# Nearest-neighbour upsampling by two: four equal loads replaced by eight that grow from 1 MiB to 4 MiB

## The chip, the cores and the metric

The kernel runs on one core of a Trainium2 chip, with nothing else running. The metric is the device time of one execution in microseconds (us); quoted times are medians of several runs. All runs quoted here were fast ones, with a granted clock of 1.0 (the share of full TensorE speed that the profile lists), so they may be compared with each other. A difference under 2% counts as "the same".

## The reference

Every element of a 16 x 64 x 64 x 64 array of 32-bit floats is repeated twice in both image directions:

```
result[:, :, i, j] = x[:, :, i // 2, j // 2]     # out: 16 x 64 x 128 x 128
```

There is no arithmetic. The kernel must read 16.78 MB and write 67.11 MB.

## The kernel before

The image rows are cut into four blocks of 128 partitions x 128 rows. A block is loaded by one DMA of 4 MiB: each partition receives one contiguous run of 32 KiB. All four loads are issued at the start, into four buffers. Then each block is expanded in four steps of 32 rows: VectorE writes 18 of the rows, ScalarE 14, into one of two output buffers of 4 MiB, and one store sends it to HBM, again as one contiguous 32 KiB run per partition.

```
K, J = 32, 4
NB = R // (P * J * K)                       # 4 blocks
xpool = ctx.enter_context(tc.tile_pool(name="xin", bufs=NB))
upool = ctx.enter_context(tc.tile_pool(name="uexp", bufs=2))

for n in range(NB):
    xt = xpool.tile([P, J * K, W], fdt, name="xt")
    nc.sync.dma_start(out=xt[:, :, :], in_=xf[n])                    # L67
    xts.append(xt)

for n in range(NB):
    for j in range(J):
        r0 = j * K
        u = upool.tile([P, K, s, W, s], fdt, name="u")
        nc.vector.tensor_copy(out=u[:, :KV], in_=expanded(...))      # L78
        nc.scalar.copy(out=u[:, KV:], in_=expanded(...))             # L81
        nc.sync.dma_start(out=of[n, :, r0 : r0 + K, :], in_=u[...])  # L84
```

Loads and stores are all issued by SyncE, so they all go into one DMA queue, in program order. (The first load is moved in front of the barrier with which the program begins; the change leaves that alone.)

## Time and profile before

| | before |
|---|---|
| time, median of 3 runs | 199.99 us (199.93 to 200.45) |
| span in the profile | 198.2 us |
| DMA queue, share of 16 engines' span | 98.8% |
| VectorE (DVE) / ScalarE (ACT) busy | 21% / 26% |
| VectorE waits for the first load | 12.3 us |

The first thing to read is the page: the busy time of the engines; then the span in 40 equal slices, where each digit is the busy share in tenths (9 is 90% or more); then the DMA packets and the one queue.

```profile
DVE 40.9 (21%) x16; ACT 52.0 (26%) x17; POOL 0.2 (0%) x4
...
DVE  0055000000405050505050505050505050404000
ACT  2057000000415150606060606060606060505000
...
DMA  8999999999999999999999999999999999999994
...
DMA packets 2880, 83.89 MB, mean 423 GB/s; under 512 B 320, under 2 KB 320, under 8 KB 320
...
q1 hardware_dynamic: 2880, 83.89, 98.8%
```

The DMA row is full from the first slice to the last; the two compute engines mostly have nothing to do. Their early digits (slices 3 and 4) are the first two outputs, made at 12 to 19 us. Then both engines stop for 33 us. The waits (engine, line, what it waited for, us in total, times, longest us) and the timeline (start, duration, engine, line, what) of the kernel before say why:

```profile
DVE u L78 <- DMA out_dram<-u: 127.3, 14, 34.7
ACT u L81 <- DMA out_dram<-u: 118.0, 14, 33.5
DVE u L78 <- DMA xt<-in_x_dram: 12.3, 1, 12.3
```

```profile
0.00 2.15 SPq L67 DMA_DIRECT2D xt<-in_x_dram  x4
...
15.55 40.05 SPq L84 DMA_DIRECT2D out_dram<-u  x3
```

All four loads are in the queue at 2.15 us. The first store is issued at 15.55 us, behind all of them, and lands at 52.0 us; only then is an output buffer free again. The copies are waiting for the stores, and the stores for the DMA engines.

The chain that ended last, followed in order of time (start, us, what):

```profile
0.00 12.32 DMA xt<-in_x_dram
...
12.35 6.27 ACT u L81 x2
...
18.63 43.02 DMA out_dram<-u
...
64.96 16.04 DMA out_dram<-u
```

It begins with a wait of 12.32 us for the first load. Its next transfer is a store that takes 43.02 us to land where later ones take 16.04, and most of it is time in the queue behind loads.

The trace's packet records give durations. On each of the 16 DMA engines, packets of 32 KiB take 1,213 ns, one behind the other, in the load stage as in the store stage.

### The profile page before, as it was taken

How to read it: one execution, taken by the hardware profiler on the slowest of the kernel's cores; microseconds unless marked ns; L12 is line 12 of the kernel's file. 1: busy time of each engine (PE TensorE's matmuls, PEld its weight loads, DVE VectorE, ACT ScalarE, POOL GpSimd, SP SyncE). 2: the span in 40 equal slices, each digit the busy share in tenths (PEclk: the TensorE clock that was granted, in tenths of full speed). 3: DMA queues.
4: the chain of work that ended last, by engine and by line, in shares of the span. 5: the costliest groups of instructions: out<-in, count | busy, mean ns of one | idle time of the engine just before them, and what ended most of it. 6: DMA issues, size and time to landing. Idle time of an engine off the chain costs nothing.

```text
span 198.2 us, 145 instructions
## 1 busy us (share of the span) xinstructions
DVE 40.9 (21%) x16; ACT 52.0 (26%) x17; POOL 0.2 (0%) x4
## 2 busy tenths in 40 slices
DVE  0055000000405050505050505050505050404000
ACT  2057000000415150606060606060606060505000
POOL 0000000000000000000000000000000000000000
DMA  8999999999999999999999999999999999999994
GB/s 317 423 423 430 450 430 456 370 403 423 423 423 436 436 443 456 436 436 423 423 423 423 423 443 443 450 450 436 423 423 423 423 423 436 436 443 456 436 436 212
DMA packets 2880, 83.89 MB, mean 423 GB/s; under 512 B 320, under 2 KB 320, under 8 KB 320
## 3 DMA queue, kind: packets, MB, share of 16 engines
q1 hardware_dynamic: 2880, 83.89, 98.8%
HBM read 16.78 MB, written 67.11 MB: 423 GB/s over the span
## 4 chain that ended last, share of the span: by engine, by line
DMA 77%; ACT 14%; issue 0%; ACTq 0%
DMA out_dram<-u 70%; ACT u L81 14%; DMA xt<-in_x_dram 6%; ACTq L81 0%
## 5 line engine op out<-in xcount | busy, mean ns | idle before, releaser
L81 ACT COPY u<-xt 128x3584 f32<-128x3584 f32 x16 | 50.8, 3179 | 128.3 <-DMA out_dram<-u 118.0
L78 DVE COPY u<-xt 128x4608 f32<-128x4608 f32 x16 | 40.9, 2560 | 139.6 <-DMA out_dram<-u 127.3
L81 ACT ACT_TABLE_LOAD x1 | 1.3, 1283 | 0.8 <-PEq L103 0.8
L103 POOL MEMSET const-bfloat16-1.0<- 128x1 bf16 x1 | 0.1, 102 | 0.0
L103 POOL MEMSET const-uint8-127<- 128x1 uint8 x1 | 0.1, 102 | 0.0
L103 POOL MEMSET const-float32-0.0<- 128x1 f32 x1 | 0.1, 99 | 0.2 <-issue 0.2
L103 POOL MEMSET const-float32-1.0<- 128x1 f32 x1 | 0.1, 99 | 0.0
## 6 DMA issues: line engine op xcount, KB each, us to landing
out_dram<-u SPq DMA_DIRECT2D x16, 4096.0 KB, 16.1
xt<-in_x_dram SPq DMA_DIRECT2D x4, 4096.0 KB, 25.9
```

The source lines that it names most:

```text
L78: nc.vector.tensor_copy(out=u[:, :KV], in_=expanded(xts[n][:, r0 : r0 + KV, :]))
L81: nc.scalar.copy(out=u[:, KV:], in_=expanded(xts[n][:, r0 + KV : r0 + K, :]))
L103: nc = _bacc.Bacc("TRN2", target_bir_lowering=False, num_devices=1)
```

## The change

The intent is to let the first copies and the first store start earlier, by making the first loads small (1 MiB, 8 KiB per partition), and to keep the large 32 KiB runs for the last two loads. Core of the diff:

```
+    blocks = [32, 32, 32, 32, 64, 64, 128, 128]      # rows per partition
-    K, J = 32, 4
+    K = 32
...
-    xpool = ctx.enter_context(tc.tile_pool(name="xin", bufs=NB))
+    xpool = ctx.enter_context(tc.tile_pool(name="xin", bufs=1))
...
-    for n in range(NB):
-        xt = xpool.tile([P, J * K, W], fdt, name="xt")
-        nc.sync.dma_start(out=xt[:, :, :], in_=xf[n])
-        xts.append(xt)
+    for n, k in enumerate(blocks):
+        xt = xpool.tile([P, k, W], fdt, name=f"x{n}")     # its own buffer each
+        nc.sync.dma_start(out=xt[:, :, :], in_=of_block(xf, first, k))
+        loaded.append((xt, first, k))
+        first += P * k
...
+    for xt, first, k in loaded:
+        for r0 in range(0, k, K):
             ...                                           # copies and stores as before
```

More of the change, by code (lines that the diff above doesn't have):

```diff
@@ L44 @@
     fdt = x.dtype
-    K, J = 32, 4
-    NB = R // (P * J * K)
-    assert NB * P * J * K == R
-    xf = x.rearrange("b c h w -> (b c h) w").rearrange(
-        "(n p r) w -> n p r w", n=NB, p=P
-    )
-    of = out.rearrange("b c (h hd) w -> (b c h) (hd w)", hd=s).rearrange(
-        "(n p r) w -> n p r w", n=NB, p=P
-    )
-    KV = 18
-    xpool = ctx.enter_context(tc.tile_pool(name="xin", bufs=NB))
-    upool = ctx.enter_context(tc.tile_pool(name="uexp", bufs=2))
-    xts = []
-    for n in range(NB):
-        xt = xpool.tile([P, J * K, W], fdt, name="xt")
-        nc.sync.dma_start(out=xt[:, :, :], in_=xf[n])
-        xts.append(xt)
@@ L70, in expanded, with of_block @@
-    def expanded(rows):
-        k = rows.shape[1]
-        return rows.unsqueeze(2).unsqueeze(4).to_broadcast([P, k, s, W, s])
-    for n in range(NB):
-        for j in range(J):
-            r0 = j * K
+    blocks = [32, 32, 32, 32, 64, 64, 128, 128]
+    K = 32
+    assert P * sum(blocks) == R
+    KV = 18
+    xf = x.rearrange("b c h w -> (b c h) w")
+    of = out.rearrange("b c (h hd) w -> (b c h) (hd w)", hd=s)
+    def of_block(rows, first, k):
+        return rows[first : first + P * k, :].rearrange("(p k) w -> p k w", p=P)
@@ new lines @@
+    xpool = ctx.enter_context(tc.tile_pool(name="xin", bufs=1))
+    upool = ctx.enter_context(tc.tile_pool(name="uexp", bufs=2))
+    loaded = []
+    first = 0
+    for n, k in enumerate(blocks):
[3 more added lines that the diff above has]
+        first += P * k
+    def expanded(rows):
+        return rows.unsqueeze(2).unsqueeze(4).to_broadcast(
+            [P, rows.shape[1], s, W, s]
+        )
@@ L77 @@
+    for xt, first, k in loaded:
+        for r0 in range(0, k, K):
             u = upool.tile([P, K, s, W, s], fdt, name="u")
             nc.vector.tensor_copy(
-                out=u[:, :KV], in_=expanded(xts[n][:, r0 : r0 + KV, :])
+                out=u[:, :KV], in_=expanded(xt[:, r0 : r0 + KV, :])
             )
             nc.scalar.copy(
-                out=u[:, KV:], in_=expanded(xts[n][:, r0 + KV : r0 + K, :])
+                out=u[:, KV:], in_=expanded(xt[:, r0 + KV : r0 + K, :])
@@ L83 @@
             )
             nc.sync.dma_start(
-                out=of[n, :, r0 : r0 + K, :], in_=u[:, :, :, :, :]
+                out=of_block(of, first, k)[:, r0 : r0 + K, :],
+                in_=u[:, :, :, :, :],
             )
```

## The prediction

> **What bounds the kernel.** The DMA engines, from first to last microsecond. The page gives one queue with 98.8% of 16 engines' span, 83.89 MB at 423 GB/s over 198.2 us; VectorE and ScalarE are busy 21% and 26%. The trace's packet records show how full that is: each engine moves 160 packets of 32 KiB back to back at 1,213 ns (16 x 32 KiB / 1.213 us = 432 GB/s), and 20 completion packets of 9 ns. The Trainium skill ("DMA: Bandwidth & Descriptors", "Where 436 GB/s comes from") puts the fabric's ceiling at 435 GB/s; the trace agrees within 1%. What is not transfer at this pace is small: 1.0 to 2.0 us before each engine's first packet, up to 1.1 us more in that packet, about 1.1 us in slower packets at 38 to 40 us, where loads give way to stores, and about 1.5 us after the last packet.
>
> **Loads do not interleave with stores.** All four loads are issued by 2.2 us (timeline), the first store at 15.6 us, on the same queue. The same page ("Queues, rings and completion order") says that each engine takes descriptors in ring order. The trace agrees: the second store, issued at 18.6 us, takes 43.0 us to land (chain of waits), since it stands behind the 16.8 MB of loads; later ones take 16.1 us. So the 12.3 us that VectorE waits for the first load (waits) costs nothing: the DMA engines are full meanwhile, and the first two outputs lie ready over 20 us before the queue reaches them. The chain lists that wait, but its next piece, the 43.0 us store, is mostly queueing.
>
> **What the change does.** Bytes, stores, buffers and copies stay the same. On SyncE the order stays all loads, then all stores; eight loads replace four. The first load is 1 MiB instead of 4. I expect it to land at about 5 us instead of 12.3 (8 packets of about 0.3 us, after 1 to 2 us to the start and the first-packet delay), the first store to be issued at about 9 instead of 15.6 us, and to queue longer by as much. None of these 7 us is on the path that sets the time.
>
> Costs: load packets per engine go from 32 to 64 (32 of 8 KiB, 16 of 16 KiB, 16 of 32 KiB), completion packets from 20 to 24. If each of these 36 more costs what a completion packet takes, 9 ns, they cost 0.3 us (estimate). Four more issues of about 0.4 us on SyncE stay ahead of the transfers.
>
> **Prediction: 200.3 us, range 199.7 to 201.0.** Faster by over 2%: 0.01; within 2%: 0.97; slower by over 2%: 0.02.
>
> **What the profile would show.** If right: DMA again 98 to 99%; 3,456 packets; VectorE's wait for the first load about 5 us; its longest wait for a store grows from 34.7 to about 41 us; the first store still lands near 52 us; later stores still 9.7 us apart; 8 KiB packets at 303 to 312 ns. Wrong, if an 8 KiB packet takes over 330 ns, if there are gaps between loads, or if stores overtake loads.
>
> **What would make it wrong.** A larger cost per descriptor: 8 KiB packets at 350 ns would add 1.5 us. A queue too deep (eight loads and two stores outstanding, against four and two) that leaves engines dry. A transition from loads to stores that costs another amount than 1.1 us. A gain over 1 us would need the start-up or the transition to shrink.

## The result, and the profile after

| | before | after |
|---|---|---|
| time, median of 4 runs | 200.01 us | 200.04 us |
| span in the profile | 198.2 us | 198.2 us |
| VectorE waits for the first load | 12.3 us | 4.9 us |
| first store issued | 15.55 us | 8.15 us |
| last load lands | 42.27 us | 42.52 us |
| first store lands | 51.97 us | 52.20 us |
| last store lands | 197.15 us | 197.40 us |

The ratio is 0.9998, with a 95% interval of 0.9981 to 1.0016: the same. Landings are read from the trace's semaphore events, counted from the start of the span.

The page of the changed kernel:

```profile
DVE 40.9 (21%) x16; ACT 52.1 (26%) x17; POOL 0.2 (0%) x4
...
DVE  0900000000404050505050505050505050504000
ACT  2920000000424151506060606060606060605000
...
DMA  7999999999999999999999999999999999999995
...
DMA packets 3456, 83.89 MB, mean 423 GB/s; under 512 B 384, under 2 KB 384, under 8 KB 384
...
q1 hardware_dynamic: 3456, 83.89, 98.8%
```

The first two outputs moved from slices 3 and 4 to slice 2, as intended. The DMA row, the mean rate and the queue's share did not move. Now its waits, and the beginning of its chain in order of time:

```profile
DVE u L80 <- DMA out_dram<-u: 134.9, 14, 42.4
...
DVE u L80 <- DMA x<-in_x_dram: 4.9, 1, 4.9
```

```profile
0.00 4.92 DMA x<-in_x_dram
...
4.94 3.19 ACT u L83
...
8.15 44.05 DMA out_dram<-u
```

The wait for the load shrank by 7.4 us, and the longest wait for a store grew by 7.7 us, from 34.7 to 42.4. The first store is issued 7.4 us earlier and lands 0.2 us later.

### The profile page after: what moved, and what is told of

Read it like the earlier page. It is cut to its first block, busy times and chain, and to the rows that moved or that the text cites. A ratio compares the mean times of both kernels' runs of the same rounds, so it can differ in the third digit from the quotient of the medians.

```text
span 198.2 us, 155 instructions
## 1 busy us (share of the span) xinstructions
DVE 40.9 (21%) x16; ACT 52.1 (26%) x17; POOL 0.2 (0%) x4
## 2 busy tenths in 40 slices
DMA packets 3456, 83.89 MB, mean 423 GB/s; under 512 B 384, under 2 KB 384, under 8 KB 384
## 3 DMA queue, kind: packets, MB, share of 16 engines
q1 hardware_dynamic: 3456, 83.89, 98.8%
## 4 chain that ended last, share of the span: by engine, by line
DMA 73%; ACT 14%; another core or an unknown queue 3%; issue 0%; ACTq 0%
DMA out_dram<-u 71%; ACT u L83 14%; DMA x<-in_x_dram 2%; ACTq L83 0%
## 5 line engine op out<-in xcount | busy, mean ns | idle before, releaser
L83 ACT COPY u<-x 128x3584 f32<-128x3584 f32 x16 | 50.8, 3179 | 128.5 <-DMA out_dram<-u 125.6
L80 DVE COPY u<-x 128x4608 f32<-128x4608 f32 x16 | 40.9, 2560 | 139.9 <-DMA out_dram<-u 134.9
```

Source lines behind the costliest of these rows:

```text
L80: nc.vector.tensor_copy(out=u[:, :KV], in_=expanded(xt[:, r0 : r0 + KV, :]))
L83: nc.scalar.copy(out=u[:, KV:], in_=expanded(xt[:, r0 + KV : r0 + K, :]))
```

## The experiments

Theory A: the DMA queue always holds work, so the moment at which the first load lands is worth nothing; only engine time counts (packets, idle engines). Its main rival B: the early start does save several us, and the smaller packets cost as much again, so that the two cancel. All numbers on single packets come from the packet records of one profile per kernel; I found out which packets belong to one engine by joining each packet's end to the next one's start.

### The early first load without small packets, and the reverse

Three kernels take the two halves of rival B apart. In the first, the changed kernel's list is turned round: the same packets, but a late first load.

```
-    blocks = [32, 32, 32, 32, 64, 64, 128, 128]
+    blocks = [128, 128, 64, 64, 32, 32, 32, 32]
```

> The changed kernel with its list of blocks reversed (128, 128, 64, 64, 32, 32, 32, 32): same eight loads and the same packets, but the first load is 4 MiB again. Theory A (the DMA queue is never empty, so when the first load lands does not matter; only packets and idle engine time count): the first load lands near 12.3 us instead of 4.9, the first store is issued near 15.5 us, the last load lands near 42.5 us, and the time is that of the changed kernel, 199.9 to 200.4 us. Rival B (the early first load does save several us, and smaller packets give them back): slower than the kernel before by 3 us or more.

Measured: 199.58 us (199.53 to 199.63), ratio to before 0.9978 (0.9965 to 0.9990). Its waits show that the first load is late again:

```profile
DVE u L80 <- DMA out_dram<-u: 127.3, 14, 34.8
...
DVE u L80 <- DMA x<-in_x_dram: 12.1, 1, 12.1
```

Losing the early first load cost nothing, so rival B falls on this side. The kernel even came out 0.4 us below both, just outside what theory A had foreseen; that is taken up further down.

In the second, only the first load is small:

```
-    blocks = [32, 32, 32, 32, 64, 64, 128, 128]
+    blocks = [32, 96, 128, 128, 128]
```

> Only the first load small (blocks 32, 96, 128, 128, 128): the early first load with 32, 24 and 32 KiB packets behind it, so nearly none of the cost of small packets. Theory A: first load at 4.9 us, first store issued near 8 us, time 199.8 to 200.3 us, the same as before. Rival B: faster than before by 3 us or more.

Measured: 200.24 us (200.17 to 200.35), ratio 1.0011 (0.9999 to 1.0024). The first load landed at 4.74 us. The early start by itself gains nothing.

In the third, the kernel before keeps its four loads, but a gap after every 32 rows on chip cuts each run into four of 8 KiB:

```
-        xt = xpool.tile([P, J * K, W], fdt, name="xt")
-        nc.sync.dma_start(out=xt[:, :, :], in_=xf[n])
+        xt = xpool.tile([P, J, K * W + 16], fdt, name="xt")
+        nc.sync.dma_start(out=xt[:, :, : K * W],
+                          in_=xf[n].rearrange("p (j k) w -> p j (k w)", j=J))
```

> The kernel before with the four 4 MiB loads cut into 8 KiB packets (64 bytes of padding after every 32 rows on chip), first load at 12.3 us as before: the supposed cost alone, without the benefit. Theory A: from the changed kernel's packets (309 ns for 8 KiB, 1213 for 32 KiB, each start 3.5 ns before the end of the last) one packet more costs about 4 ns; 96 more per engine cost 0.4 us: 200.2 to 200.7 us. Rival B: 3 us or more slower.

Measured: 200.09 us (199.99 to 200.14), ratio 1.0003 (0.9990 to 1.0015), a little under the expected range. So there was no loss of several us that could have cancelled a gain. From the changed kernel's packets the cost can be read directly: 8, 16 and 32 KiB take 309, 611 and 1,213 ns, each starting 3 to 4 ns before the end of the one before, which leaves a straight line of 37.7 ns per KiB plus 4.6 ns per packet. The changed kernel's 32 extra load packets per engine are then worth 0.15 us, and the 96 of this third kernel 0.44 us. Its time rose by only 0.1 us: in its profile, the packets before the turn from loads to stores were slowed by 0.84 us less than in the kernel before, while the first packets started 0.26 us later (both are in the table further down).

### Much smaller pieces

To be sure that such a cost would be seen, the same trick with a gap after every two rows cuts the loads into pieces of 512 bytes:

```
-        xt = xpool.tile([P, J * K, W], fdt, name="xt")
-        nc.sync.dma_start(out=xt[:, :, :], in_=xf[n])
+        xt = xpool.tile([P, J * K // 2, 2 * W + 8], fdt, name="xt")
+        nc.sync.dma_start(out=xt[:, :, : 2 * W],
+                          in_=xf[n].rearrange("p (g k) w -> p g (k w)", k=2))
 ...        # each copy in two, one for each of the two output rows
```

> The kernel before with the four loads cut into 512-byte packets (32 bytes of padding after every two rows; each copy in two halves): 2048 load packets per engine in place of 32. A straight extension of 4 ns per packet gives 2016 x 4.2 ns = 8.5 us more, 208 to 210 us, and 512-byte packets of about 27 ns. If small packets cost more than the straight line says, the time is over 212 us. In both cases the loss has to be in the load stage, before the last load lands, with stores still 9.7 us apart.

Measured: 215.95 us (215.82 to 215.99), ratio 1.0795 (1.0779 to 1.0812). The straight line was wrong: the loads lost 15.9 us (the last one landed at 58.14 us instead of 42.27), which over 2,016 extra pieces per engine is 7.9 ns apiece and not 4. The trace lumps 16 such pieces into one record of 8 KiB, of typically 436 ns against 309. The stretches of time below (bounds in us, length, busy time of VectorE, ScalarE and GpSimd, clock, DMA share, GB/s) are first those of this kernel, then those of the kernel before:

```profile
5.00:55.00 50.00, 9.93 (x4) 6.45 (x4) 0.00 (x0) 1.00 1.01 303
65.00:190.00 125.00, 65.16 (x26) 42.53 (x26) 0.00 (x0) 1.00 1.00 432
```

```profile
5.00:40.00 35.00, 5.03 (x2) 6.26 (x2) 0.00 (x0) 1.00 1.03 434
65.00:190.00 125.00, 30.72 (x12) 38.15 (x12) 0.00 (x0) 1.00 1.00 432
```

The DMA engines are fully busy in all four rows; in the load stage alone they move less, 303 GB/s against 434. A DMA share of 100% therefore does not say that bytes move at full pace: both columns have to be read. (Each piece is followed by a gap of 32 bytes on chip, so most pieces do not start at a multiple of 512 bytes there; whether that has a part in the cost was not tested.)

### When the queue is not filled ahead

Here the loads are held back until they are needed, with one input buffer instead of one per load, so that each load must wait for the copies of the block before. The same edit is made to the kernel before (four loads) and to the changed one (eight):

```
-    xpool = ctx.enter_context(tc.tile_pool(name="xin", bufs=NB))
+    xpool = ctx.enter_context(tc.tile_pool(name="xin", bufs=1))
-    (all loads ahead of the loop)
     for n in range(NB):
+        xt = xpool.tile([P, J * K, W], fdt, name="xt")
+        nc.sync.dma_start(out=xt[:, :, :], in_=xf[n])
```

> The kernel before with one input buffer: a load can start only when the copies of the block before are done, so loads are no longer queued ahead and the queue runs dry once a block. Theory A: each of the four loads leaves the DMA engines idle from its landing through the copy (3.2 us) and the issue of a store (1 to 2 us to its first packet), some 4.5 to 5.5 us, against none after the start in the kernel before: 4 x 5 = 20 us more, 216 to 224 us, with about 5 us of low DMA share after each load. Rival B says nothing against this; it is the yardstick for the next run.

> The changed kernel's blocks with one input buffer (eight loads, first one 1 MiB). Theory A: idle time is counted per load, eight times some 5 us, 234 to 246 us, so the smaller first loads make it slower by some 20 us than the same kernel with four large loads, although the first store is issued 7 us earlier. Rival B, that an earlier first store shortens the time where nothing is queued ahead: at most as slow as the four loads with one buffer, or faster by up to 7 us.

Measured: 221.68 us with four loads (ratio 1.1079, 1.1064 to 1.1093) and 244.08 us with eight (ratio 1.2198, 1.2182 to 1.2214), both within theory A's ranges. Stretches of the kernel with four loads:

```profile
2.00:12.00 10.00, 0.00 (x0) 0.06 (x1) 0.00 (x0) 1.00 0.85 367
12.00:16.00 4.00, 3.77 (x2) 3.77 (x2) 0.00 (x0) 1.00 0.00 0
16.00:64.00 48.00, 6.38 (x3) 8.85 (x3) 0.00 (x0) 1.00 1.01 426
66.00:70.00 4.00, 3.42 (x2) 3.44 (x2) 0.00 (x0) 1.00 0.00 0
```

And of the one with eight:

```profile
4.00:8.50 4.50, 2.56 (x1) 3.18 (x1) 0.00 (x0) 1.00 0.01 5
9.00:22.00 13.00, 0.00 (x0) 0.00 (x0) 0.00 (x0) 1.00 0.91 363
22.00:26.50 4.50, 2.56 (x1) 3.18 (x1) 0.00 (x0) 1.00 0.00 0
```

After each load, while its first rows are copied, no engine moves anything. The packet records hold four such holes of 4.40 to 4.53 us in the first kernel and eight of 4.44 to 4.57 us in the second; in the kernel before there is none after the first packet. The holes sum to 18.0 and 36.1 us, most of the 21.6 and 44.0 us lost. Counted for each DMA engine by itself, the added idle time is 19.4 and 38.1 us, and packets slower than usual grew from 1.6 us per engine to 4.0 and 7.5 us; together these make up nearly all of the 21.7 and 44.2 us by which the mean engine ended later. The second kernel issues its first store 7.5 us before the first one does (at 7.97 us against 15.44) and ends 22.4 us after it. Time is lost by each interval in which the queue is empty, and not by a late start.

### Loads among the stores

Two kernels keep the queue filled but break up the order "all loads, then all stores". In the first, each load is issued one block ahead of its use:

```
+    load(0)
     for n, (xt, first, k) in enumerate(loaded):
+        if n + 1 < len(loaded):
+            load(n + 1)                 # blocks = [128, 128, 128, 128]
```

> Four 4 MiB loads, but each load is issued one block ahead only, so that it stands in the queue among stores: three changes from stores to loads and back in place of one. Theory A: engines stay full, so 200 us plus what further changes between reading and writing HBM cost; the one change in the kernel before costs 0.97 us of slower packets per engine, so two to four more of them, 200.5 to 204 us. If a change of direction costs nothing as such (the slow packets are peculiar to the first store), 199.8 to 200.3 us.

Measured: 201.13 us, with an unusual spread (200.43 to 202.73), ratio 1.0057 (1.0024 to 1.0090): within the first of the two expected ranges. In its profile packets were stretched by 1.9 us per engine in all, against 1.6 before; but the mean engine ended only 0.4 us later, and the slowest 1.65 us later. The sixteen engines of a store landed within 0.6 us of each other in the kernel before; here within 0.9 to 1.2 us before the last load, and within 2.0 us after it and to the end. So the loss in that profile is mainly one of engines falling apart; that this is what happens at every turn was not tested. The time fell into the range by another way than the one it was worked out from: all the extra turns together cost 0.3 us of slower packets per engine, and not 0.97 us each.

In the second, the changed kernel's loads, all but the first, go into ScalarE's queue, so that stores need not stand behind them:

```
-        nc.sync.dma_start(out=xt[:, :, :], in_=of_block(xf, first, k))
+        q = nc.scalar if n else nc.sync
+        q.dma_start(out=xt[:, :, :], in_=of_block(xf, first, k))
```

> The changed kernel with all loads but the first issued on the ScalarE queue, so that loads and stores no longer stand in one line: the first store should land near 15 to 30 us instead of 52 us. Theory A: engines are as full as before, so 199.5 to 201.5 us although stores start 25 to 35 us earlier. Rival C (the early first load would pay if stores did not have to stand behind the loads): faster by 3 us or more.

Measured: 201.61 us (201.35 to 202.40), ratio 1.0083 (1.0067 to 1.0099). Its waits, and its two DMA queues (packets, MB, share of 16 engines):

```profile
DVE u L81 <- DMA out_dram<-u: 136.4, 14, 19.2
...
DVE u L81 <- DMA x<-in_x_dram: 4.9, 1, 4.9
```

```profile
q1 hardware_dynamic: 2448, 68.16, 79.4%
q10 hardware_dynamic: 1008, 15.73, 19.1%
```

The longest wait for a store fell from 42.4 to 19.2 us, and the first store landed at 26.95 us instead of 52.20. The time became 1.6 us longer, a little beyond the expected range. In its profile the mean engine ended 0.9 us later than in the kernel before and the slowest 1.6 us later, so part of the loss is again engines falling apart; its cause was not tested. This rules out rival C of that run, that the early load would pay if only the stores did not stand behind the loads: the two queues share the same DMA engines, and 79.4% and 19.1% together are 98.5%, against 98.8% before. (The first store was issued at 9.19 us here and not at 8.15, since ScalarE issued seven loads before its first copy. Two queues with a late first load were not run.)

### The 0.4 us of the reversed list

The reversed list gave 199.58 us. In the kernel before, the last two load packets of each engine, before the turn to stores, are stretched from 1,213 to 1,513 and 1,881 ns on average, 0.97 us in all; with 8 KiB packets throughout it was 0.13 us, and in the reversed list 0.56 us. From that I formed theory T: the stretch belongs to the size of the last packets before the turn. Four kernels tested it, three of them the kernel before with a gap after every 32 rows in one load alone (c = 3, 0 and 2):

```
+        pad = 16 if n == c else 0
+        xt = xpool.tile([P, J, K * W + pad], fdt, name=f"x{n}")
```

and one the changed kernel with `blocks = [128, 128, 128, 96, 32]`.

> The kernel before with only the fourth load cut into 8 KiB packets (padding after every 32 rows), all else alike. In the kernel before the last two load packets of each engine are stretched from 1213 to 1513 and 1881 ns on average, 0.97 us in all; with 8 KiB packets all through the stretch was 0.13 us. Theory T (the stretch belongs to the size of the last packets before the turn from loads to stores): some 0.5 to 0.8 us less stretch, 0.1 us more for 24 extra packets, so 199.2 to 199.6 us and the last load landing at 41.5 to 41.9 us instead of 42.3. Rival (the 0.4 us gain of the reversed list came from something else, such as the first packets): 199.9 to 200.2 us.

> The changed kernel with blocks 128, 128, 128, 96, 32: large first loads, one small 1 MiB load last. Theory T: 199.4 to 199.7 us, as the reversed list (199.58). Rival (the gain of the reversed list needs four small loads, or comes from elsewhere): 199.9 to 200.2 us.

> The kernel before with only the first load cut into 8 KiB packets. Theory T: nothing gained at the turn; 24 packets more per engine cost 0.1 us, and the first packets start some 0.2 us later (with all four loads cut the mean start was 1.54 us against 1.28): 200.1 to 200.5 us, first load landing at 12.5 to 12.8 us. Rival (position does not matter): the same as with the last load cut.

> Control: only the third load cut into 8 KiB packets, so that neither the first nor the last packets change. Theory T: 24 packets more at 4 ns, 0.1 us: 200.0 to 200.3 us, stretch of the last two load packets 0.9 to 1.1 us as in the kernel before. Rival: under 199.8 us.

The table gives the medians and ratios, and per-engine means worked out from each profile's packet records: the start of the first packet, how far packets at the turn were stretched beyond their usual length, and the end of the last data packet of the mean engine (all in us).

| kernel | time | ratio (95% interval) | mean start | stretch at the turn | mean end |
|---|---|---|---|---|---|
| before | 199.99 | | 1.28 | 0.97 | 196.55 |
| changed | 200.04 | 0.9998 (0.9981 to 1.0016) | 1.47 | 0.88 | 196.62 |
| reversed list | 199.58 | 0.9978 (0.9965 to 0.9990) | 1.27 | 0.56 | 196.35 |
| all four loads in 8 KiB | 200.09 | 1.0003 (0.9990 to 1.0015) | 1.54 | 0.13 | 196.62 |
| last load in 8 KiB | 199.97 | 0.9998 (0.9984 to 1.0011) | 1.30 | 0.79 | 196.52 |
| last block small | 199.97 | 0.9998 (0.9986 to 1.0011) | 1.22 | 0.70 | 196.50 |
| first load in 8 KiB | 200.30 | 1.0014 (1.0001 to 1.0026) | 1.67 | 0.67 | 196.81 |
| third load in 8 KiB | 199.82 | 0.9993 (0.9980 to 1.0005) | 1.29 | 0.62 | 196.34 |

Theory T fell. Cutting the last load gained nothing, nor did a small last block, though both were expected to gain 0.3 to 0.8 us; with the last load cut, that load landed at 42.32 us and not at 41.5 to 41.9. The control, whose last packets are those of the kernel before, had a stretch of only 0.62 us and came out under its expected range. Only the run with the first load cut came out in its expected range: its packets start 0.4 us later on the mean engine, and the time grew by 0.3 us; but its stretch at the turn was smaller too, 0.67 us, where theory T saw no gain there. Each row rests on one profile, and no kernel was profiled twice, so the stretch may also differ from one execution to the next; that was not tested. What sets it, and so why the reversed list is 0.2% faster than the kernel before, stays open. No version beat both kernels by an amount that matters.

## Why the prediction was right

- The bound. DMA engines full from end to end: 98.8% before and after.
- The queue order. No store overtook a load; the first store landed at 52.20 us, predicted near 52. The 7.4 us by which the first store is issued earlier went into a longer time in the queue: the longest wait for a store grew to 42.4 us (predicted about 41; the first store was issued at 8.15 us, where I had put about 9).
- The Trainium skill, page "DMA: Bandwidth & Descriptors", section "Queues, rings and completion order", says that each engine works through its ring in order, and that rings of several queues take turns on the same engine. The trace agrees on both: in order within one queue here; with a second queue, packets of the two alternated one for one on an engine from about 14 us, and the first store landed at 26.95 us, for a total that was 1.6 us longer and not shorter.
- The cost of smaller packets. 3,456 packets as predicted; 309 ns for 8 KiB lies in the range given. The term of 0.3 us (36 packets at 9 ns) was too large: a load packet costs 4.6 ns beyond its bytes, which makes 0.15 us for the 32 of them. This is an error of size that is smaller than what moved at the turn. In the profile the mean engine ended 0.07 us later and the slowest 0.24 us later; the span grew by 0.01 us.
- The turn from loads to stores. The prediction counted about 1.1 us of slower packets there; it is 0.97 us, and they are the last load packets, not stores. It was listed as a thing that could upset the forecast, and it is indeed the largest part that moved between otherwise equal kernels, by some tenths of a us, for reasons I could not find.
- The time. 200.04 us against 200.3, inside 199.7 to 201.0.

## What to carry to other kernels

When the DMA row is full from the first slice to the last, an engine's wait for the first load need not be a cost, and was none here, even though the chain of waits begins with it: ask what the DMA engines do during that wait, and what the saved time will stand behind. Moving transfers to an earlier place in a queue that is never empty changed who waited for whom and left the total where it was (199.99 and 200.04 us); what counted was the number of bytes, the pace per packet, and every interval in which the queue was empty, here 4.4 to 4.6 us for each load that was not issued ahead. A cost per piece measured on large pieces should not be extended in a straight line to small ones: it was 4.6 ns at 8 to 32 KiB and 7.9 ns at 512 bytes.

## What the Trainium skill lacked or had wrong

- "DMA: Bandwidth & Descriptors", "Specifications": 512 bytes is given as the smallest transfer for line rate. Loads cut into 512-byte runs, with gaps of 32 bytes between them on chip, moved 303 GB/s here, against 434 GB/s with 32 KiB runs in the same stage.
- The same page, "Where 436 GB/s comes from": it says that for transfers between HBM and on-chip memory the HBM side, about 358 GB/s, is the limit, though it calls its own 425 GB/s for 16 MB near the fabric's rate. With one core alone the loads ran at 434 GB/s and the stores at 432 GB/s, within 1% of the 435 GB/s given for the fabric. "HBM Reference", "Specifications (TRN2)", has this right in kind, with about 425 GB/s for a core alone.
- The same page, "Measured": 341 GB/s for a transfer of 1 MiB issued from GpSimd. Loads of 1 MiB issued from SyncE and queued behind one another landed 2.46 to 2.50 us apart here, which is 420 to 426 GB/s; the page does not say what queueing does to its figure.
- No page that I read has the cost of the turn from loads to stores: the last load packets of each engine were stretched by 0.13 to 1.12 us in all, and kernels with the same last packets differed (0.97 and 0.62 us).
